# Layer norms with epsilon and negative mean on VectorE, one half tile on ScalarE, and three more modulations of layer 2 on TensorE

## The chip, the cores and the metric

The kernel runs on one core of a Trainium2 chip. The metric is the time of one execution in device microseconds. PE is TensorE (matmuls and transposes), DVE is VectorE, ACT is ScalarE, POOL is GpSimd, SP is SyncE, whose queue starts nearly all the transfers.

## The reference, cut to what matters

Four layers with four different mixers (pool, attention, a state-space model, a gated MLP) on a latent stream of 256 rows by 1024; in the first two layers a context stream of the same size goes through the same steps. Every layer norm normalises rows over 1024 columns, and every layer has six modulation vectors, each a product of a conditioning vector with a 1024 x 1024 matrix.

```python
def layer_norm(x, g, b):
    mu = jnp.mean(xf, axis=-1, keepdims=True)
    var = jnp.mean(jnp.square(xf - mu), axis=-1, keepdims=True)
    y = (xf - mu) * lax.rsqrt(var + LN_EPS) * g + b
...
for layer in range(DEPTH):                       # pool, attn, ssm, gmlp
    sh1, sc1, gt1, sh2, sc2, gt2 = jnp.split(silu(c) @ ada_w[layer] + ada_b[layer], 6)
    h_lat = modulate(x_lat, sh1, sc1)            # x * (1 + sc) + sh; h_ctx the same with c_ctx
    y_lat, y_ctx = mixer(h_lat, h_ctx)
    x_lat = layer_norm(ALPHA * x_lat + gt1 * y_lat, ln1_g, ln1_b)
    f_lat = conv_ffn(modulate(x_lat, sh2, sc2))
    x_lat = layer_norm(ALPHA * x_lat + gt2 * f_lat, ln2_g, ln2_b)
    # x_ctx goes through the same two norms in layers 0 and 1
```

## The kernel before, in words

The rows of the streams lie on the partitions in tiles `xa0` to `xa3` of 128 x 1024: tiles 0 and 1 are one stream, 2 and 3 the other. Layers 0 and 1 work on four tiles (`S=2`), layers 2 and 3 on two (`S=1`).

**Matmuls.** Every product is three matmuls of split operands, `mm3` (L229 to L231). A weight arrives by DMA as `raw`, ACT writes its high part `wH` (L170), and DVE, in some places POOL, its low part `wL` (L171).

**Modulations.** `ada_task(l, m)` makes modulation m of layer l (0 shift, 1 scale, 2 gate, 3 to 5 the same for the FFN). It loads eight slabs `araw` of 128 x 1024 (L327, issued from SP's queue, three buffers). Where `array(l, m)` holds, PE multiplies each slab straight from `araw` in `products` (L320): eight matmuls of 128 x 32 by 128 x 256, four column groups in two passes; it does so two slabs behind the load (`lag`). Otherwise DVE multiplies the slab by one column of the condition and adds it to an accumulator `adaS` (L337 for the first slab, L339 for the other seven), and PE sums `adaS` over the partitions at the end with one such group of eight. A gate adds a group for its bias. The tasks are background work of the matmul loops: some are advanced at each weight slab. Those of layer 2 with m = 0 to 4 run during the FFN of layer 1, about 855 to 1110 us; m = 0 and 1 already go to PE, m = 2, 3 and 4 to DVE.

**Second half of the two large FFNs.** While the FFN of layer 0 and again that of layer 1 go on, POOL builds tables for the state-space layer, group by group (`ef`, `efp`, L1176 to L1183, 128 x 512), which PE reads as background work (L1387, L1406). For layer 0's FFN this is 318 to 518 us, for layer 1's 977 to 1179 us.

**Layer norms.** `stats` collects sums per tile while the last matmuls of a stage land. `post(t, S)` then takes `rstd`: `bn_aggr` on DVE (mean and variance, L538), variance plus epsilon (L540) and the power of -0.5 (L541) on POOL. With `S=2` POOL goes on: the negative mean (L609), then both halves of the tile, `(x + nm) * rs` (L612). With `S=1` POOL makes `nm = -mean * rs` (L605), and `norm` runs the halves on ACT (L498, needs `nm`) and on DVE (L500, needs mean and `rs`). After that PE transposes the tile (`turn`, L555, or `turn_tile`, L506), and ACT and DVE modulate it into `hH`, `h` and `hL` (`modulate`, L582 to L591, or `modulate_tile`, L522 to L528). `finish` and the gated MLP's own norm use `rstd` too. The norms that `post` handles are the two of layers 0 and 1 (16 tiles), the two of layer 2 and the first of layer 3 (6 tiles).

**Order.** Each engine works through its queue in order. The order of DVE, ACT, POOL and SP is made by a planner that simulates a timeline, except inside `manual_schedule` blocks, where it is the order of the program. The whole pool layer is such a block. There `post(3)` comes ahead of `need((l, 3))` and `mod_coeffs` (L409 to L412, the coefficients `mA`, `mB` of `modulate`).

Of the kernel before, what the change touches and what calls it, by code (L numbers as in the profile page):

```python
# [7 lines left out]
F32 = mybir.dt.float32  # L8
# [3 lines left out]
ALU = mybir.AluOpType  # L12
# [9 lines left out]
EPS = 1e-5  # L22
# [43 lines left out]
class Trunk:  # L66
# [232 lines left out]

    def array(self, l, m):  # L300

        return l < 2 or l == 2 and m < 2

# [185 lines left out]
    def norm(self, t, engs):  # L491

        nc = self.nc
        mean, rs, nm = self.norms[t]
        for hf, e in enumerate(engs):
            x = self.xa[t][:, hf * 512:hf * 512 + 512]
            if e is nc.scalar:
                e.activation(x, x, AF.Identity, scale=rs, bias=nm)  # L498
            else:
                e.tensor_scalar(x, x, mean, rs, op0=ALU.subtract, op1=ALU.mult)  # L500

    def turn_tile(self, t):

# [30 lines left out]
    def rstd(self, st):  # L534

        nc = self.nc
        mv = self.t(self.sm, [128, 2], F32, "mv", 4)
        self.last_mv = nc.vector.bn_aggr(mv, st.rearrange("p a b -> p (a b)"))  # L538
        rs = self.t(self.sm, [128, 1], F32, "rs", 4)
        nc.gpsimd.tensor_scalar(rs, mv[:, 1:2], EPS, 1.0, op0=ALU.add, op1=ALU.mult)  # L540
        self.last_norm = nc.gpsimd.tensor_tensor(rs, rs, self.half, op=ALU.pow)  # L541
        return mv[:, 0:1], rs

# [55 lines left out]
    def post(self, t, S=2):  # L599

        G = self.nc.gpsimd
        mean, rs = self.rstd(self.st[t])
        if S == 1:
            nm = self.t(self.sm, [128, 1], F32, "nm", 4)
            G.tensor_scalar(nm, mean, rs, -1.0, op0=ALU.mult, op1=ALU.mult)  # L605
            self.norms[t] = mean, rs, nm
            return
        nm = self.t(self.sm, [128, 1], F32, "nm", 4)
        G.tensor_scalar(nm, mean, -1.0, 1.0, op0=ALU.mult, op1=ALU.mult)  # L609
        for hf in range(2):  # L610
            x = self.xa[t][:, hf * 512:hf * 512 + 512]
            self.last_norm = G.tensor_scalar(x, x, nm, rs, op0=ALU.add, op1=ALU.mult)  # L612

    def post_T(self, coef):

# [226 lines left out]
    def out_proj_steps(self, l, w, n_k, gates, norm, S, lhs, lead=0):  # L842


        NT = 2 * S
        made = {}
        def end():
            made["g"] = gates()
            made["n"] = norm()
        for hf in range(2):  # L850
            c0 = hf * 512
            P = 2 if S == 1 and hf else 1
            if hf:
                self.conv(l)
            if hf and S == 2:
                ahead = self.ahead([w for w, shape in self.first_up(l, 2)])
            def close(t, p, ps):
                if not made:
                    end()
                self.add_gated(t, c0 + p * 256, ps, made["g"][t // 2])  # L860
                if hf == 1 and p == P - 1:
                    self.post(t, S)
            yield from self.project_steps([(w[:, k:k + 2, c0:c0 + 512], (k, k + 1)) for k in range(0, n_k, 2)],
                                          lambda k, t: lhs(k, slice(t * 128, t * 128 + 128)), (0, n_k - 1), NT, 3 if hf else 0, P, close,
                                          made["n"][0] if P == 2 else None,
                                          self.first_up(l) if P == 2 and self.extra else (), 0 if hf else lead,
                                          (lambda: made["n"][0]) if S == 2 and hf else None)
        if S == 2:
            self.early = ahead
            self.post_T(made["n"][0])  # L870
        self.post_x(range(NT), made["n"][1])
# [813 lines left out]
    def gmlp_layer(self, l):  # L1685
# [5 lines left out]
        with ExitStack() as later:  # L1691
# [39 lines left out]
            for cp in range(8):  # L1731
# [7 lines left out]
                for j in range(2):  # L1739
# [12 lines left out]
                    for t in range(2):  # L1752
# [3 lines left out]
                    self.split(nH[:, :, cs], nL[:, :, cs], gt)  # L1756
            norm = self.pre_ln1(l)
            self.out_proj(self.out_proj_steps(l, I["gmlp_w_out"][0].rearrange("(k p) n -> p k n", p=128), 16, lambda: gates, lambda: norm, 1,
                          lambda k, ts: (nH[:, ts.start // 128, k * 128:k * 128 + 128], nL[:, ts.start // 128, k * 128:k * 128 + 128])))

# [229 lines left out]
```

## Time and profile before

| | |
|---|---|
| median of 3 runs | 1935.31 us (1934.91 to 1938.88) |
| the profiled execution's own time | 1940.46 us |
| its span in the trace | 1938.7 us |
| mean granted clock of PE | 0.96 |
| DVE busy | 1318.2 us (68%) |
| ACT busy | 781.3 us (40%) |

The profiled execution is one run of its own; its time lies 5.15 us above the median of the others. Durations of the trace belong to it. An engine's busy time is an average over stages that have different limits.

### The profile page before, as it was taken

What the parts mean: (1) busy time and instruction counts of PE and PEld (TensorE: products, weight loads), DVE (VectorE), ACT (ScalarE), POOL (GpSimd) and SP (SyncE); (2) the same over time, 40 slices, a digit from 0 to 9 for tenths busy, and PEclk for the clock granted to TensorE, in tenths of its full rate; (3) what the DMA queues carried; (4) which work ended last, traced back from release to release, by engine and by line L of the source; (5) the groups of instructions that cost most, each with busy time, mean ns of one, the idle gap of its engine ahead of it and who ended that gap; (6) DMA issues with size and microseconds to landing.
All of it is one profiled execution on the core that took longest, in us unless ns stands there. A gap on an engine that the chain in (4) does not pass through costs nothing.

```text
span 1938.7 us, 31709 instructions
## 1 busy us (share of the span) xinstructions
PE 1782.9 (92%) x12188; PEld 1466.6 (76%) x12188; DVE 1318.2 (68%) x1853; ACT 781.3 (40%) x1289; POOL 1080.3 (56%) x1040
## 2 busy tenths in 40 slices
PE   6899999899999999999989998688899988979997
PEld 4687676677789878777767776458798878979997
DVE  4565545546677767654676747987879798778666
ACT  2253223224346644422422332234654454436553
POOL 2278104989862335751189998647654444246643
PEclk8899999999999999999989999889899989989999
DMA  9555565565321124566656556865878765547662
GB/s 365 185 156 183 174 190 181 197 206 184 121 87 38 45 80 100 180 189 187 210 194 220 177 186 207 250 222 182 267 273 276 254 222 186 171 154 262 205 188 85
DMA packets 241785, 360.28 MB, mean 186 GB/s; under 512 B 43353, under 2 KB 164825, under 8 KB 241634
## 3 DMA queue, kind: packets, MB, share of 16 engines
q1 hardware_dynamic: 241634, 358.26, 57.2%
q8 instruction: 96, 1.57, 0.3%
q14 instruction: 55, 0.45, 0.1%
HBM read 330.92 MB, written 27.29 MB: 185 GB/s over the span
## 4 chain that ended last, share of the span: by engine, by line
PE 56%; POOL 21%; DVE 11%; issue 4%; DMA 4%; ACT 2%; SPq 0%; POOLq 0%; DVEq 0%; ACTq 0%
PE ps L229 15%; PE ps L230 14%; PE ps L231 14%; POOL ef L1178 2%; DVE wL L171 2%; POOL efp L1182 2%; POOL ef L1181 2%; POOL ef L1183 2%; POOL cv L1824 2%; POOL ef L1176 2%; POOL efp L1177 2%; PE sc L991 1%; PE ps L939 1%; PE ada L320 1%; PE pv L1046 1%
## 5 line engine op out<-in xcount | busy, mean ns | idle before, releaser
L171 DVE TENSOR_TENSOR wL<-raw,wH 128x1024 fp32r<-128x1024 f32 x292 | 422.8, 1453 | 197.2 <-ACT wH L170 189.9
L229 PE MATMUL ps<-hH,wH 128*128 128x256 f32 (+1 forms) x1568 | 524.2, 335 | 9.9 <-ACT wH L170 5.5
L170 ACT ACTIVATE wH<-raw 128x1024 fp32r<-128x1024 f32 x341 | 358.2, 1056 | 419.2 <-PE ps L231 218.3
L231 PE MATMUL ps<-hH,wL 128*128 128x256 f32 (+1 forms) x1568 | 516.8, 330 | 4.5 <-DVE wL L171 4.5
L230 PE MATMUL ps<-hL,wH 128*128 128x256 f32 (+1 forms) x1568 | 518.0, 331 | 1.6 <-DVE hL L528 1.1
L229 PEld LDWEIGHTS ps<-hH,wH 128*128 128x128 f32 x1568 | 301.7, 193 | 52.1 <-issue 8.9
L231 PEld LDWEIGHTS ps<-hH,wL 128*128 128x128 f32 x1568 | 301.5, 193 | 31.3 <-DVE wL L171 4.8
L230 PEld LDWEIGHTS ps<-hL,wH 128*128 128x128 f32 x1568 | 302.6, 193 | 26.7 <-POOL xa L633 1.3
L1824 POOL TENSOR_TENSOR cv<-cv,cv 128x512 f32<-128x512 f32 (+1 forms) x88 | 110.2, 1257 | 224.8 <-ACT cv L1823 224.8
L229 PE MATMUL ps<-wH,gH 128*128 128x512 f32 (+1 forms) x552 | 220.6, 400 | 9.0 <-DVE cv L1796 7.2
L231 PE MATMUL ps<-wH,gL 128*128 128x512 f32 (+1 forms) x552 | 213.9, 392 | 2.4 <-POOL gL L1828 2.3
L230 PE MATMUL ps<-wL,gH 128*128 128x512 f32 (+1 forms) x552 | 215.8, 391 | 0.0
L171 POOL TENSOR_TENSOR wL<-raw,wH 128x1024 fp32r<-128x1024 f32 x49 | 127.2, 2596 | 110.1 <-ACT wH L170 90.0
L1793 ACT ACTIVATE cv<-ps,cw 128x512 f32<-128x512 f32 (+1 forms) x176 | 115.9, 666 | 164.1 <-PE ps L231 138.9
L1794 DVE SCALAR_TENSOR_TENSOR cv<-ps,cw,cv 128x510 f32<-128x510 f32 (+1 forms) x176 | 106.5, 609 | 106.1 <-ACT cv L1793 105.9
L339 DVE SCALAR_TENSOR_TENSOR adaS<-araw,cond,adaS 128x1024 f32<-128x1024 f32 x70 | 117.0, 1671 | 36.2 <-DMA araw<-in_ada_w_dram 36.0
L229 PEld LDWEIGHTS ps<-wH,gH 128*128 128x128 f32 x552 | 106.0, 192 | 41.1 <-issue 15.8
L231 PEld LDWEIGHTS ps<-wH,gL 128*128 128x128 f32 x552 | 105.8, 192 | 26.8 <-POOL gL L1828 3.3
L230 PEld LDWEIGHTS ps<-wL,gH 128*128 128x128 f32 x552 | 106.1, 192 | 21.0 <-issue 0.2
L1796 DVE SCALAR_TENSOR_TENSOR cv<-ps,cw,cv 128x510 f32<-128x510 f32 (+1 forms) x176 | 106.7, 612 | 4.3
L540 POOL TENSOR_SCALAR rs<-mv 128x1 f32<-128x1 f32 x26 | 8.2, 314 | 165.5 <-DVE mv L538 165.0
L1827 ACT ACTIVATE gH<-cv 128x512 fp32r<-128x512 f32 (+1 forms) x88 | 45.9, 521 | 117.6 <-POOL cv L1824 117.6
(434 smaller groups left out, 3322.9 us busy)
## 6 DMA issues: line engine op xcount, KB each, us to landing
araw<-in_ada_w_dram SPq DMA_DIRECT2D x184, 512.0 KB
raw<-in_ffn_w_up_dram SPq DMA_DIRECT2D x176, 512.0 KB
raw<-in_ffn_w_down_dram SPq DMA_DIRECT2D x88, 512.0 KB
raw<-in_gmlp_w_in_dram SPq DMA_DIRECT2D x32, 512.0 KB
fD<-ef SPq DMA_DIRECT2D x16, 512.0 KB
eD<-eo SPq DMA_DIRECT2D x16, 512.0 KB
raw<-in_gmlp_w_out_dram SPq DMA_DIRECT2D x16, 512.0 KB
raw<-in_attn_w_qkv_dram SPq DMA_DIRECT2D x12, 512.0 KB
```

Source lines behind the costliest of these rows:

```text
L170: self.nc.scalar.activation(h, x, AF.Copy)
L171: (eng or self.nc.vector).tensor_tensor(l, x, h.bitcast(F32), op=ALU.subtract)
L229: mm(ps, lhsT=w[0], rhs=x[0], start=first, stop=False)
L230: mm(ps, lhsT=w[0], rhs=x[1], start=False, stop=False)
L231: mm(ps, lhsT=w[1], rhs=x[0], start=False, stop=last)
L339: nc.vector.scalar_tensor_tensor(a, raws[k], self.cond[:, k, r:r + 1], a, op0=ALU.mult, op1=ALU.add)
L1176: eng.tensor_tensor(out[0], a[0], b[0], op=ALU.mult)
L1793: nc.scalar.activation(c, p3, AF.Identity, scale=cw[:, 1, h:h + 1], bias=cw[:, 3, h:h + 1])
L1794: nc.vector.scalar_tensor_tensor(c[:, :, 1:], p3[:, :, :255], cw[:, 0, h:h + 1], c[:, :, 1:], op0=ALU.mult, op1=ALU.add)
L1796: nc.vector.scalar_tensor_tensor(c[:, :, :255], p3[:, :, 1:], cw[:, 2, h:h + 1], c[:, :, :255], op0=ALU.mult, op1=ALU.add)
L1824: nc.gpsimd.tensor_tensor(cv[0, j], cv[0, j], cv[1, j], op=ALU.mult)
L1827: nc.scalar.activation(gH, c0, AF.Copy)
```

## The change

1. `array`: modulations m = 2, 3 and 4 of layer 2 are now multiplied on PE from `araw`.
2. `rstd`: epsilon is added on DVE, with one instruction fewer for POOL; the power stays on POOL.
3. `post`: `nm = -mean * rs` is made on DVE, behind the power, for every tile, also with `S=2`. With `S=2` the halves go through `norm`: POOL with mean and `rs`, and ACT with `rs` and `nm` for the first half of tile 3.

```diff
     def array(self, l, m):
-        return l < 2 or l == 2 and m < 2
+        return l < 2 or l == 2 and m < 5
...
     def norm(self, t, engs):
...
-                e.tensor_scalar(x, x, mean, rs, op0=ALU.subtract, op1=ALU.mult)
+                i = e.tensor_scalar(x, x, mean, rs, op0=ALU.subtract, op1=ALU.mult)
+                if e is nc.gpsimd:
+                    self.last_norm = i
...
     def rstd(self, st):
...
-        nc.gpsimd.tensor_scalar(rs, mv[:, 1:2], EPS, 1.0, op0=ALU.add, op1=ALU.mult)
+        nc.vector.tensor_scalar(rs, mv[:, 1:2], EPS, None, op0=ALU.add)
         self.last_norm = nc.gpsimd.tensor_tensor(rs, rs, self.half, op=ALU.pow)
...
     def post(self, t, S=2):
         G = self.nc.gpsimd
         mean, rs = self.rstd(self.st[t])
-        if S == 1:
-            nm = self.t(self.sm, [128, 1], F32, "nm", 4)
-            G.tensor_scalar(nm, mean, rs, -1.0, op0=ALU.mult, op1=ALU.mult)
-            self.norms[t] = mean, rs, nm
-            return
         nm = self.t(self.sm, [128, 1], F32, "nm", 4)
-        G.tensor_scalar(nm, mean, -1.0, 1.0, op0=ALU.mult, op1=ALU.mult)
-        for hf in range(2):
-            x = self.xa[t][:, hf * 512:hf * 512 + 512]
-            self.last_norm = G.tensor_scalar(x, x, nm, rs, op0=ALU.add, op1=ALU.mult)
+        self.nc.vector.tensor_scalar(nm, mean, rs, -1.0, op0=ALU.mult, op1=ALU.mult)
+        self.norms[t] = mean, rs, nm
+        if S == 2:
+
+            self.norm(t, (self.nc.scalar if t == 3 else G, G))
```

## Rows read from the trace of the kernel before

**Rows 1.** The page, part 1: busy time, share and instructions of each engine.
```profile
PE 1782.9 (92%) x12188; PEld 1466.6 (76%) x12188; DVE 1318.2 (68%) x1853; ACT 781.3 (40%) x1289; POOL 1080.3 (56%) x1040
```

**Rows 2.** Busy time by stretch, equal parts of two FFNs: PE, PEld, DVE, ACT, POOL, PEclk, DMA.
```profile
269.90:498.70 228.80, 221.39 (x1530) 165.14 (x1530) 116.57 (x120) 79.51 (x118) 167.51 (x127) 0.99 0.59 188
928.10:1161.60 233.50, 215.13 (x1370) 167.58 (x1368) 153.82 (x145) 77.17 (x116) 179.35 (x127) 0.96 0.59 197
```

**Rows 3.** The same view of line L230 alone: the two stretches.
```profile
269.90:498.70 228.80, 105.17 (x267) 50.53 (x267) 0.99 0.59 188
928.10:1161.60 233.50, 107.51 (x267) 52.17 (x267) 0.96 0.59 197
```

**Rows 4.** The chain that ended last within each of the two stretches.
```profile
by line: PE ps L229 18.5%; PE ps L230 17.2%; PE ps L231 17.2%; POOL ef L1178 5.7%; PE ada L320 4.4%; POOL ef L1181 4.2%; POOL ef L1176 4.0%; POOL ef L1183 3.9%; POOL efp L1182 3.4%; DMA prm<-prmD 3.3%; POOL cv L1824 2.9%; DMA prmD<-big 2.8%
...
by line: POOL ef L1178 12.1%; POOL efp L1182 11.5%; POOL ef L1181 10.1%; POOL efp L1177 9.8%; POOL ef L1183 9.6%; POOL ef L1176 8.3%; DMA prm<-prmD 6.7%; POOL cv L1824 5.7%; PE ps L229 4.6%; PE ps L230 4.3%; PE ps L231 4.3%; DMA araw<-in_ad
```

**Rows 5.** Line L339 alone, in one stretch: time, DVE busy (instructions).
```profile
935.00:1182.00 247.00, 34.87 (x21) 0.96 0.57 192
```

**Rows 6.** Groups of line L320: the sums over partitions for layer 2's modulations.
```profile
L320 PE MATMUL ada<-adaS,ones x24: 379/391/404, 987.7 to 1109.2; 128*32 128x256 f32 x24
```

**Rows 7.** PE in order of time around one slab of a modulation.
```profile
905.42 0.39 PE L230 MATMUL ps<-hL,wH 128*128 128x512 f32 x1
905.65 0.39 PE L231 MATMUL ps<-hH,wL 128*128 128x512 f32 x1
905.97 0.64 PE L320 MATMUL ada<-araw,cond 128*32 128x256 f32 x8
...
906.87 0.39 PE L230 MATMUL ps<-hL,wH 128*128 128x512 f32 x1
```

**Rows 8.** One line of POOL's table work over the whole kernel: ns minimum/median/maximum.
```profile
L1182 POOL TENSOR_TENSOR efp<-prm x40: 1045/1396/2068, 329.5 to 1176.5; 128x512 f32<-128x512 f32 x40
```

**Rows 9.** Waits of SP's queue in the first stretch: total us, times, longest.
```profile
SPq L327 <- PE ada L320: 39.3, 14, 4.5
```

**Rows 10.** All engines in order of time: first norm of layer 0, tile 3.
```profile
78.12 0.17 DVE L409 TENSOR_SCALAR ada<-ada 128x16 f32<-128x16 f32 x1
...
78.46 2.34 POOL L171 TENSOR_TENSOR wL<-raw,wH 128x1024 fp32r<-128x1024 f32 x1 [4.64 <-ACT wH L170]
78.61 2.21 DVE L412 TENSOR_TENSOR mB<-mB,ada 128x16 f32<-128x16 f32 x1
...
80.86 3.76 ACT L582 ACTIVATE hH<-ps,mB,mA 128x256 fp32r<-128x256 f32 x8 [2.49 <-DVE mB L412]
81.90 0.19 POOL L540 TENSOR_SCALAR rs<-mv 128x1 f32<-128x1 f32 x1
...
82.17 0.55 POOL L541 TENSOR_TENSOR rs<-rs,half 128x1 f32<-128x1 f32 x1
...
87.76 0.55 PE L229 MATMUL ps<-hH,wH 128*128 128x256 f32 x1 [1.13 <-DVE h L588]
```

**Rows 11.** POOL and DVE in order of time: second norm of layer 0, tile 3.
```profile
536.28 1.03 POOL L540 TENSOR_SCALAR rs<-mv 128x1 f32<-128x1 f32 x1 [3.36 <-DVE mv L538]
537.40 1.05 POOL L609 TENSOR_SCALAR nm<-mv 128x1 f32<-128x1 f32 x1
538.41 1.53 POOL L541 TENSOR_TENSOR rs<-rs,half 128x1 f32<-128x1 f32 x1
540.05 1.52 POOL L612 TENSOR_SCALAR xa<-xa,nm,rs 128x512 f32<-128x512 f32 x2
...
536.11 3.43 DVE L171 TENSOR_TENSOR wL<-raw,wH 128x1024 fp32r<-128x1024 f32 x3
```

**Rows 12.** First norm of layer 3, tile 1, in order of time.
```profile
1721.68 0.66 DVE L522 TENSOR_SCALAR h<-ps,mA,mB 128x128 f32<-128x128 f32 x2
1722.72 0.55 DVE L500 TENSOR_SCALAR xa<-xa,mv,rs 128x512 f32<-128x512 f32 x1 [0.38 <-POOL rs L541]
...
1723.32 0.66 PE L506 MATMUL ps<-ident,xa 128*128 128x128 f32 x4 [2.03 <-DVE xa L500]
```

## Prediction

> **What bounds the kernel now.** I read the page first. PE is busy for 1782.9 of 1938.7 us, 92%, far ahead of DVE's 68% and POOL's 56% [rows 1]. So over the whole kernel PE is nearly the limit, and work added to PE costs time unless it falls into gaps that PE has anyway. The share is a mean over stages, though, and part 1 of the change acts in one stage, the second half of layer 1's FFN. So the second view is busy time by stretch. I laid two stretches of equal work beside each other: from the 900th to the 100th of the main matmuls counted from the FFN's end, once in layer 0's FFN and once in layer 1's. That they are equal is seen on one of the three products: 267 instructions of L230 in both [rows 3]. POOL has 127 instructions in both, table work for the state-space layer for the most part [rows 2]. What differs is the modulations. In layer 0's stretch all of them are on PE, so PE has 1530 instructions against 1370: 160 more, which are 20 slabs of eight. In layer 1's stretch those of m = 2, 3 and 4 are on DVE: 145 DVE instructions against 120, 153.82 us busy against 116.57. And yet layer 0's stretch is the shorter one: 228.80 us against 233.50 [rows 2]. The third view, the chain that ended last, says why: in layer 0's stretch three lines of matmuls lead it with 53% together, in layer 1's six lines of POOL's tables with 61% [rows 4]. In layer 1's stretch PE is idle for 18.37 us (233.50 less 215.13), in layer 0's for 7.41, and it is granted 0.96 of its clock against 0.99 [rows 2]. In layer 1's stretch PE waits for POOL, and POOL is slower there: 179.35 us busy for 127 instructions against 167.51, 11.84 more.
>
> The reader is to see that layer 0's stretch is a picture of layer 1's after the change, in the same trace.
>
> **Part 1, modulations from DVE to PE.** Removed: 24 DVE instructions of 128 x 1024 (three of L337, and the 21 of L339, which take 34.87 us of DVE [rows 5]), and three of PE's groups of eight over `adaS` [rows 6]. Added: 24 groups of eight on PE, one for each slab. Net: 21 groups more. What a group costs where PE is never idle, one place shows: from the start of one matmul of the main stream at 905.65 to the one two behind it at 906.87 is 1.22 us with a group between; without one, a step of this stream is 0.23 us (905.42 to 905.65), two are 0.46. The group costs 0.76 us [rows 7], and 21 of them 16.0 us: the upper bound of part 1.
>
> By the Trainium skill ("TensorE: Matmul & The Clock Gate", Part 3: Packing small matmuls) matmuls on different column tiles run side by side, so that four of them last about as long as one; by that rule the two passes of a group are worth two matmuls, and with half the columns of a main one that is about one step of the stream, 0.23 us, as an estimate 4.8 us for 21. The row says 0.76 us, and the row decides. The same section says that a weight load overlaps matmuls under way only where the row group differs, which speaks against this form, as the four column tiles share their rows.
>
> The lower bound: POOL sets the pace throughout, and gets rid of what DVE's large operations cost it. One line of its tables takes 1045 ns at the least and 2068 at the most with the same shape [rows 8], so an overlap can double it; the 11.84 us of busy time between the stretches [rows 2] is the total. So the ends are -11.84 and +16.0. Between these ends I go by the nearest row, which is the layer 0 stretch itself: -4.70 us. It has 20 groups more, the change adds 21; one more at the rate at which PE's busy time grew (221.39 less 215.13 over 20, 0.31 us) makes **-4.4 us**. That stretch also includes what the change does to the queues: with PE two slabs behind, SP's queue waits for PE to free an `araw`, 39.3 us in 14 waits [rows 9], with weight loads queued behind it. It is the shorter stretch all the same, with the DMA engines at 0.59 in both [rows 2].
>
> **Parts 2 and 3, the layer norms.** POOL loses an epsilon and an `nm` for each tile, 0.19 us apiece where nothing disturbs them [rows 10], and DVE gets both at about the same price (0.17 to 0.19 us, its smallest rows). The price that matters is another one: `nm` on DVE waits for POOL's power, and DVE takes its queue in order, so everything behind `nm` waits about 0.9 us: power 0.55, `nm` 0.19, epsilon 0.19.
>
> *First norm of layer 0, tile 3.* The order is the program's: `nm` stands ahead of the coefficients L409 to L412. Before, DVE did L409 at 78.12, and L412 ended at 80.82, when POOL's L171, which stands ahead of the power, had let it go; ACT's `hH` began at 80.86 [rows 10]. After, the power still waits for POOL's L171 and the instruction behind it (to 81.82), begins at 81.90, epsilon's place, and ends at 82.45; `nm` is done at about 82.7; the coefficients, at 0.17 each, at about 83.5. So `hH` begins 2.7 us later, and at the end of that chain PE stands idle for DVE's `h` at 87.76 [rows 10]. The half on ACT makes the tile itself earlier, but it is the coefficients that are late next. Bounds 0 and +3; I take **+2.5**, as the chain on DVE behind it has no gap.
>
> *Second norm of layer 0, tile 3.* Epsilon 1.03, `nm` 1.05, power 1.53 and then two halves: POOL is held by three L171 of DVE at the same time [rows 11]. After, epsilon is 0.19 on DVE, `nm` leaves POOL's chain and one half of 0.76 goes to ACT: 0.84 + 1.05 + 0.76 = 2.65 less. Against it, the three L171, low parts of weights, start about 1.1 us later behind `nm`. Bounds -3 and 0; I take half, **-1.3**. The second norm of layer 1 has the same shape with no contention (0.19 + 0.19 + 0.76 less, some 0.4 of it lost to the wait): -0.7. The first norm of layer 1 lies under matmuls: +0.2, to +1 without that cover.
>
> *The norms with `S=1`.* Here `nm` comes ahead of two L522 that DVE did while it waited: they ran at 1721.68, and L500 waited 0.38 us for the power at 1722.72 [rows 12]. After, the pair starts at about 1722.9, when the power (which L500 saw end just ahead of 1722.72) and `nm` are done, and L500 at 1723.55, 0.8 later; PE waits for just that instruction (2.03 us) [rows 12]. ACT gets `nm` earlier, but PE needs both halves: +0.7. Two other places have this shape, the first and second norm of layer 2; worked the same way, with the wait of tile 0 in it, they give +1.0 and +0.45. Together **+2.2**, bounds 0 and +4. The gated MLP's own norm and the last one only lose the epsilon on POOL, which there lies under a DVE operation: -0.5 and -0.3.
>
> Sum of the norms: 2.5 - 1.3 - 0.7 + 0.2 + 2.2 - 0.8 = **+2.1 us**.
>
> **Sum.** -4.4 + 2.1 = -2.3 us. The profiled execution took 1940.46 us (span 1938.7, 1.76 around it); it becomes 1938.2. It is 5.15 above the median of the runs shown, so against the median of 1935.31 I forecast **1933.0 us**. About 0.2%, 3.9 us, is what a measurement of this kernel can tell from no change.
>
> **Rivals.**
>
> *1. PE sets the pace and the groups aren't absorbed (slower).* For it: PE is at 92% over the kernel, and layer 0's stretch has only 7.41 us of idle PE left, so the stage is close to PE's limit with POOL just beneath [rows 2, 4]. Its place is the main matmul stream from about 935 us on, its price 0.76 us a group [rows 7]. All 21 unabsorbed give 16.0 + 2.1 = +18.1, 1953.4 us. It decides from where the stretch is longer by 1.8 us instead of shorter by 4.4, that is where 6.2 us more of the groups stay visible than in layer 0. Against it: the 20 groups in layer 0.
>
> *2. POOL sets the pace to the end.* The 11.84 us come back, and about half of the first eight groups, which run before POOL's tables begin (8 x 0.76 = 6.1 us), is paid: -11.84 + 3.0 + 2.1 = -6.7, 1928.6 us. For it: POOL's 61% of the chain now [rows 4]. Against it: in layer 0 PE takes over before POOL's gain is used up.
>
> The Trainium skill ("SBUF — State Buffer", SBUF: two separate sides) states that DVE and GpSimd share a port pair that is locked for a whole instruction, and that the other side stops. By that rule each removed L339 could free up to its own duration, 34.9 us as an estimate for the 21; the doubling in rows 8 agrees with the rule, while the 11.84 us show that few overlaps cost that much.
>
> *3. DVE's waits at the norms are covered.* If the coefficients and the L522 had slack that I don't see, the +2.5 and the +2.2 fall away, and the norms give -2.6: -4.4 - 2.6 = -7.0, 1928.3 us. Against it: at both places PE is idle for that very chain [rows 10, 12].
>
> *4. The planner orders other work anew.* New instructions change its simulated times; work elsewhere moves by a few us either way, centred on the forecast.
>
> **How the numbers follow.** The forecast has 0.42 (its own range 1930 to 1936), rival 1 0.19, rival 2 0.20, rival 3 0.11, rival 4 0.08. Faster by over 0.2% is below 1931.4: rivals 2 and 3 for the most part, some 0.26, with the lower edge of the forecast (0.11) and a third of rival 4: 0.40. Slower is above 1939.2: rival 1 with little left out, 0.17, and part of rival 4: 0.20. The rest, 0.40, is no change that can be measured. The range from 1926.5 to 1941 leaves out most of rival 1 and the far end of rival 2.
>
> **What would show it.** In the profile after: no L339 and no L337 before 1180 us, 21 more groups of L320 there; the chain in that stretch led by matmuls and not by POOL's tables; POOL's busy time for the same 127 instructions near 167.5 us, PE's idle time near 7; the stretch itself at 229 us. At the first norm of layer 0 ACT's `hH` some 2.7 us later and PE's restart with it; at the norms with one stream L500 behind two L522 that wait for `nm`. I am wrong if that stretch is longer than 235 us, or if a wait at a norm that I have priced under 1 us turns out above 2.

## The result and the profile after

The change made the kernel slower: 1948.69 us (1947.6 to 1950.84, four runs) against 1937.1 (1934.91 to 1939.25, four runs), ratio 1.0059 with a 95% interval of 1.0042 to 1.0076, or 11.6 us. The forecast was 1933.0 us in a range from 1926.5 to 1941.0. The profiled execution took 1949.58 us with a span of 1947.8.

The line of busy times on the page of the changed kernel answers to [rows 1]:

```profile
PE 1788.5 (92%) x12356; PEld 1465.4 (75%) x12356; DVE 1285.6 (66%) x1877; ACT 786.3 (40%) x1293; POOL 1087.3 (56%) x988
```

POOL has 52 instructions fewer and is still busy 7 us longer. That is the first sign of what went wrong, as the change takes work from POOL.

Part 1 did what was forecast. In layer 1's FFN, for the same 267 instructions of L230 as in [rows 3], the views of busy time (PE, PEld, DVE, ACT, POOL, PEclk, DMA share, GB/s) and of the chain now read:

```profile
929.10:1158.30 229.20, 222.23 (x1538) 166.06 (x1538) 114.79 (x122) 78.57 (x118) 166.27 (x128) 0.99 0.63 201
by line: PE ps L229 20.8%; PE ps L230 19.2%; PE ps L231 19.2%; PE ada L320 4.2%; POOL efp L1180 4.0%; POOL ef L1176 3.8%; POOL ef L1179 3.3%; POOL ef L1181 3.1%; POOL ef L1174 2.9%; DMA prmD<-big 2.6%; POOL cv L1822 2.4%; POOL efp L1175 2.3
```

229.20 us, where the forecast was 229 and the stretch took 233.50 before [rows 2]. PE's chain leads instead of POOL's [rows 4], POOL is busy for 166.27 us instead of 179.35, and PE idle for 6.97 us instead of 18.37. The granted clock is 0.99 instead of 0.96. The picture that layer 0's stretch gave of it was right within 2 us in every engine's column; only the DMA engines are busier than there, 0.63 against 0.59.

What went wrong is on POOL, in the halves that it normalises. The view of one line, of the kernel before and of the changed one (ns minimum/median/maximum):

```profile
L612 POOL TENSOR_SCALAR xa<-xa,nm,rs x32: 757/770/1356, 56.0 to 1194.3; 128x512 f32<-128x512 f32 x32
...
L500 POOL TENSOR_SCALAR xa<-xa,mv,rs x28: 2068/2076/2551, 51.9 to 1195.0; 128x512 f32<-128x512 f32 x28
```

A half tile takes POOL 2.08 us, and took 0.77 before. With two streams the halves go through `norm` now, which subtracts the mean and multiplies, while `post` used to add a negative mean and multiply. At the second norm of layer 1 the PE waits for it. Before, POOL and PE in order of time:

```profile
1187.08 1.52 POOL L612 TENSOR_SCALAR xa<-xa,nm,rs 128x512 f32<-128x512 f32 x2
...
1190.62 0.44 PE L555 MATMUL ps<-ident,xa 128*128 128x128 f32 x2 [1.09 <-POOL xa L612]
...
1194.32 2.82 PE L555 MATMUL ps<-ident,xa 128*128 128x128 f32 x12 [2.23 <-POOL xa L612]
```

After:

```profile
1179.76 4.14 POOL L500 TENSOR_SCALAR xa<-xa,mv,rs 128x512 f32<-128x512 f32 x2
1183.86 1.44 POOL L543 TENSOR_TENSOR rs<-rs,half 128x1 f32<-128x1 f32 x2
...
1186.80 10.30 POOL L500 TENSOR_SCALAR xa<-xa,mv,rs 128x512 f32<-128x512 f32 x5
...
1188.94 1.54 PE L557 MATMUL ps<-ident,xa 128*128 128x128 f32 x6 [4.55 <-POOL xa L500]
1190.99 1.54 PE L557 MATMUL ps<-ident,xa 128*128 128x128 f32 x6 [0.51 <-POOL xa L500]
1193.05 2.74 PE L557 MATMUL ps<-ident,xa 128*128 128x128 f32 x10 [0.52 <-POOL xa L500]
1197.16 1.54 PE L557 MATMUL ps<-ident,xa 128*128 128x128 f32 x6 [1.37 <-POOL xa L500]
```

Five halves stand in a row for 10.30 us, and PE's transposes wait for one after another. (Not all of PE's 4.55 us is the operation: POOL also takes the powers of three tiles, from 1183.86 us on, ahead of these halves.) The matmul just ahead of these transposes is 4.2 us earlier than in the trace of before, the gain of part 1; at 1210 us the work stands 1.8 us later.

The trace of before held the price. The gated MLP's norm uses the subtracting form on POOL already, on 128 x 1024, and the view of its line reads:

```profile
L1726 POOL TENSOR_SCALAR v<-v,mv,rs x2: 3987/4492/4998, 1618.4 to 1622.4; 128x1024 f32<-128x1024 f32 x2
```

About 2 us for each 512 columns; the prediction didn't look there.

### The profile page after: what moved, and what is told of

Read it like the earlier page. It is cut to its first block, busy times and chain, and to the rows that moved or that the text cites. A ratio compares the mean times of both kernels' runs of the same rounds, so it can differ in the third digit from the quotient of the medians.

```text
span 1947.8 us, 32032 instructions
## 1 busy us (share of the span) xinstructions
PE 1788.5 (92%) x12356; PEld 1465.4 (75%) x12356; DVE 1285.6 (66%) x1877; ACT 786.3 (40%) x1293; POOL 1087.3 (56%) x988
## 4 chain that ended last, share of the span: by engine, by line
PE 53%; POOL 17%; DVE 13%; DMA 7%; issue 7%; ACT 2%; SPq 1%; DVEq 0%; POOLq 0%; ACTq 0%
PE ps L229 14%; PE ps L230 14%; PE ps L231 14%; DMA araw<-in_ada_w_dram 3%; DVE wL L171 3%; DVE adaS L339 2%; POOL xa L500 2%; PE ada L320 2%; PE ps L937 1%; POOL cv L1822 1%; PE sc L989 1%; POOL ef L1176 1%; POOL efp L1180 1%; PE pv L1044 1%; POOL ef L1179 1%
## 5 line engine op out<-in xcount | busy, mean ns | idle before, releaser
L171 DVE TENSOR_TENSOR wL<-raw,wH 128x1024 fp32r<-128x1024 f32 x292 | 424.2, 1457 | 232.9 <-ACT wH L170 225.1
L230 PE MATMUL ps<-hL,wH 128*128 128x256 f32 (+1 forms) x1568 | 516.8, 330 | 0.0
L230 PEld LDWEIGHTS ps<-hL,wH 128*128 128x128 f32 x1568 | 302.1, 193 | 24.1 <-issue 1.0
L230 PE MATMUL ps<-wL,gH 128*128 128x512 f32 (+1 forms) x552 | 215.0, 390 | 0.0
L171 POOL TENSOR_TENSOR wL<-raw,wH 128x1024 fp32r<-128x1024 f32 x49 | 126.7, 2588 | 114.8 <-ACT wH L170 92.0
L230 PEld LDWEIGHTS ps<-wL,gH 128*128 128x128 f32 x552 | 105.4, 191 | 20.6
L543 POOL TENSOR_TENSOR rs<-rs,half 128x1 f32<-128x1 f32 x26 | 16.7, 645 | 157.6 <-DVE rs L542 157.6
L339 DVE SCALAR_TENSOR_TENSOR adaS<-araw,cond,adaS 128x1024 f32<-128x1024 f32 x49 | 82.3, 1681 | 10.0 <-DMA araw<-in_ada_w_dram 9.9
L1014 POOL TENSOR_SCALAR araw<-araw,den 128x512 f32<-128x512 f32 (+1 forms) x64 | 40.9, 655 | 85.8 <-ACT gate L1031 24.7
```

Source lines behind the costliest of these rows:

```text
L171: (eng or self.nc.vector).tensor_tensor(l, x, h.bitcast(F32), op=ALU.subtract)
L230: mm(ps, lhsT=w[0], rhs=x[1], start=False, stop=False)
L339: nc.vector.scalar_tensor_tensor(a, raws[k], self.cond[:, k, r:r + 1], a, op0=ALU.mult, op1=ALU.add)
L1014: nc.gpsimd.tensor_scalar(pt[:, e, i], pt[:, e, i], den[:, e, i:i + 1], 1.0, op0=ALU.mult, op1=ALU.mult)
```

## The experiments

Theory A: POOL's slow operation costs the time. Theory B: PE pays for the 21 groups, rival 1 of the prediction. Each ratio is against runs of the kernel before on the same chip; where a difference in us differs from that of the medians shown, it is worked out from the ratio.

**1. Part 1 alone** (e1).

```diff
-        return l < 2 or l == 2 and m < 2
+        return l < 2 or l == 2 and m < 5
```

> Part 1 alone: modulations 2 to 4 of layer 2 on PE, everything else as before. Theory A (the norms cost the time, since POOL takes 2.07 us for a half tile in the new form instead of 0.76): this kernel is 4 to 7 us faster than before, as the stretch in layer 1's FFN gained 5 to 6 us in the trace after. Theory B (PE pays for the 21 groups): 5 to 16 us slower than before.

1936.17 us against 1938.1, ratio 0.9989 (0.9975 to 1.0002): 2 us, and not certain. Theory B is out, but A's 4 to 7 us are not there at the end either; experiments 5 and 13 turn to that.

**2. The norms alone** (e2): as after, with `m < 2` again.

> Parts 2 and 3 alone: the layer norms as after, modulations as before. Theory A: 12 to 20 us slower than before, POOL's half tiles at 2.07 us as in the trace after. Theory B: about +2 us, the sum of the prediction, whatever POOL's half tiles take, since they lie under other work.

1951.86 us, ratio 1.0063 (1.0046 to 1.0080), 12.2 us. The norms carry the whole loss.

**3. Which form is slow** (e3), in the kernel before:

```diff
...
+            if t == 0:
+                self.last_norm = G.tensor_scalar(x, x, mean, rs, op0=ALU.subtract, op1=ALU.mult)
+            elif t == 1:
+                self.last_norm = G.tensor_scalar(x, x, nm[:, 0:1], rs, op0=ALU.subtract, op1=ALU.mult)
+            elif t == 2 or hf:
+                self.last_norm = G.tensor_scalar(x, x, nm[:, 0:1], rs, op0=ALU.add, op1=ALU.mult)
+            else:
+                self.last_norm = G.tensor_scalar(x, x, rs, nm[:, 1:2], op0=ALU.mult, op1=ALU.add)
```

> The kernel before with a different form of POOL's half tile (128 x 512) for each row tile: tile 0 subtracts the mean, read from the pair of mean and variance, and multiplies; tile 1 subtracts a copy of the mean from a tile of its own; tile 2 adds the negative mean (the form of before); tile 3 multiplies first and adds second in one half, and adds first in the other. If the operation subtract is slow (A1): about 2.07 us for tiles 0 and 1, 0.76 for tile 2 and both halves of tile 3. If the operand read from the pair of mean and variance is slow (A2): 2.07 us for tile 0 alone. If any form but add first and multiply second is slow (A3): also the first half of tile 3.

The view by line, in the order of the diff:

```profile
L618 POOL TENSOR_SCALAR xa<-xa,mv,rs x8: 2075/2078/2588, 52.1 to 1194.5; 128x512 f32<-128x512 f32 x8
L620 POOL TENSOR_SCALAR xa<-xa,nm,rs x8: 2072/2082/2612, 58.2 to 1202.2; 128x512 f32<-128x512 f32 x8
L622 POOL TENSOR_SCALAR xa<-xa,nm,rs x12: 772/779/2344, 68.2 to 1206.5; 128x512 f32<-128x512 f32 x12
L624 POOL TENSOR_SCALAR xa<-xa,rs,nm x4: 772/780/937, 79.8 to 1212.1; 128x512 f32<-128x512 f32 x4
```

It is the operation (A1): 2.08 us with subtract, wherever the mean lies, and 0.78 with add, in either order. The kernel was timed once, at 1963.76 us. That is longer than experiment 6 below, which has twice as many slow halves; one run, but it suggests that what a slow half costs the kernel depends on what stands around it.

**4. Multiply, then add** (e4), in the changed kernel:

```diff
-                i = e.tensor_scalar(x, x, mean, rs, op0=ALU.subtract, op1=ALU.mult)
-                if e is nc.gpsimd:
-                    self.last_norm = i
+                if e is nc.gpsimd:
+                    self.last_norm = e.tensor_scalar(x, x, rs, nm, op0=ALU.mult, op1=ALU.add)
+                else:
+                    e.tensor_scalar(x, x, mean, rs, op0=ALU.subtract, op1=ALU.mult)
```

> The changed kernel with one edit: POOL's half tiles are x * rs + nm (multiply first, add second) instead of (x - mean) * rs. Theory A: POOL's half tiles at about 0.77 us, and the kernel comes to 1930 to 1936 us, 3 us or more below the kernel before. Theory B: no gain over the changed kernel beyond 3 us, so about 1946 us or more.

1942.16 us, ratio 1.0010 (0.9994 to 1.0026), and the halves take POOL 0.77 us again (median). Of the 11.6 us some 9.5 are gone (1.0059 less 1.0010), but it doesn't beat the kernel before, and A's 1930 to 1936 us were missed: A named the largest cost, not all of them. In its trace the stretch of layer 0's second norm (as in the table below) takes 81.7 us, over 6 us more than before; PE waits there 3.0 us for ACT's half tile, which waits for `nm`, and 2.8 us for a low part of a weight from DVE, where before the longest wait was 2.6 us. PE's granted clock is lower there as well, 0.66 from 540 to 550 us against 0.83 and 1.00 in the two traces of before; how the 6 us divide between waits and clock was not tried.

**5. The kernel before, traced again** (e5), no edit.

> The kernel before, profiled a second time, to see what two traces of one program differ by in each stretch. If stretches of a trace repeat to under 1 us, the 3 to 4 us by which the gated MLP and the last FFN differ between the traces of before and after are an effect of the order in which the planner placed other work. If they differ by 2 to 4 us between the two traces of before, they are not to be read as an effect of the change.

1936.34 us. The table below lays stretches of several traces side by side. I found the same PE instruction at both ends of each stretch in every trace, and the numbers are differences of these start times, in us; the times in the first column are rounded. Two traces of one program differ by 0 to 2.3 us in a stretch.

| stretch (times of before) | before | again | after | 1 | 2 | 4 | 6 | 8 | 11 |
|---|---|---|---|---|---|---|---|---|---|
| 49 to 110, first norm, layer 0 | 60.8 | 61.9 | 63.1 | 61.5 | 63.2 | 64.3 | 62.2 | 63.5 | 63.3 |
| 505 to 580, second norm, layer 0 | 75.0 | 74.4 | 75.9 | 74.5 | 75.5 | 81.7 | 80.9 | 75.0 | 75.0 |
| 728 to 798, first norm, layer 1 | 69.9 | 69.9 | 73.1 | 69.9 | 73.1 | 70.3 | 75.4 | 71.0 | 70.9 |
| 890 to 1160, FFN, layer 1 | 270.0 | 268.9 | 265.7 | 265.2 | 268.7 | 265.4 | 269.3 | 262.7 | 268.3 |
| 1175 to 1210, second norm, layer 1 | 35.0 | 37.3 | 41.0 | 36.0 | 41.5 | 36.1 | 43.3 | 36.0 | 35.1 |
| 1310 to 1345, first norm, layer 2 | 35.0 | 34.3 | 34.6 | 34.6 | 34.1 | 34.3 | 35.3 | 34.4 | 34.7 |
| 1545 to 1565, second norm, layer 2 | 19.8 | 19.2 | 19.4 | 20.0 | 19.9 | 20.1 | 19.9 | 19.8 | 20.1 |
| 1581 to 1640, gated MLP, layer 3 | 58.8 | 58.3 | 62.5 | 62.3 | 62.3 | 60.4 | 60.7 | 61.8 | 61.8 |
| 1735 to 1805, FFN, layer 3 | 70.0 | 70.8 | 73.5 | 74.2 | 71.8 | 70.5 | 71.8 | 72.5 | 71.9 |

**6. Subtract alone** (e6), in the kernel before:

```diff
-        nm = self.t(self.sm, [128, 1], F32, "nm", 4)
-        G.tensor_scalar(nm, mean, -1.0, 1.0, op0=ALU.mult, op1=ALU.mult)
...
-            self.last_norm = G.tensor_scalar(x, x, nm, rs, op0=ALU.add, op1=ALU.mult)
+            self.last_norm = G.tensor_scalar(x, x, mean, rs, op0=ALU.subtract, op1=ALU.mult)
```

> The kernel before with POOL's half tiles as (x - mean) * rs instead of (x + nm) * rs, and no instruction for the negative mean; epsilon and everything else as before. If POOL's subtract is what made the change slow: 32 halves of 2.07 us, 8 to 13 us slower than before. If DVE's waits at the norms made it slow: within 3 us of before.

1958.47 us against 1936.13, ratio 1.0111 (1.0089 to 1.0134), 21.5 us: twice what was expected, though one instruction for each tile is saved. 32 halves at 1.3 us more are 42 us of POOL, so about half of it is exposed. With the rest of the norms' change around it the same form costs less (12.2 us in experiment 2); there four of the halves are on ACT and epsilon doesn't queue behind POOL's halves. Which of these two does it was not tried.

**7. Add in the gated MLP's norm too** (e7), on part 1 alone:

```diff
-                    e.tensor_scalar(v, v, *norms[t], op0=ALU.subtract, op1=ALU.mult)
+                    if i:
+                        nm = self.t(self.sm, [128, 1], F32, "nm", 4)
+                        e.tensor_scalar(nm, norms[t][0], -1.0, 1.0, op0=ALU.mult, op1=ALU.mult)
+                        e.tensor_scalar(v, v, nm, norms[t][1], op0=ALU.add, op1=ALU.mult)
```

(with the old line in the `else`).

> Part 1 alone (modulations on PE, norms as before), and in the gated MLP's own norm POOL's two tiles of 128 x 1024, which subtract the mean (3.99 and 5.00 us before), add a negative mean instead. If the operation is what costs: these two at about 1.5 us each, and 3 to 6 us below the kernel with part 1 alone (1936.2 against 1938.1 before), so 4 to 8 us below before. If PE's wait there is for another engine: no gain beyond the 2 us of part 1.

1938.00 us, ratio 1.0003 (0.9988 to 1.0018): no gain. The two tiles took 2.77 and 1.72 us instead of 5.00 and 3.99, but PE's longest wait there, for ACT's `nH`, went from 3.0 us in experiment 1 to 6.1. The traces show why. In experiment 1 ACT's first `nH` waits for DVE's `v`; here it waits for POOL's, although DVE's first `v` had been done for 2 us, and PE waits behind both:

```profile
1604.94 0.81 DVE L1731 TENSOR_SCALAR v<-v,mv,rs 128x1024 f32<-128x1024 f32 x1 [0.59 <-POOL rs L541]
...
1607.82 2.00 ACT L170 ACTIVATE nH<-v 128x1024 fp32r<-128x1024 f32 x2 [5.11 <-POOL v L1729]
...
1609.88 0.47 PE L229 MATMUL ps<-wsH,nH 128*128 128x128 f32 x1 [6.08 <-ACT nH L170]
```

So ACT's order took what the cheaper instructions gave; what they are worth with the old order was not tried.

**8. POOL makes its own negative mean** (e8), in the changed kernel, so that DVE waits for the power only in tile 3 and with one stream:

```diff
-        nm = self.t(self.sm, [128, 1], F32, "nm", 4)
-        self.nc.vector.tensor_scalar(nm, mean, rs, -1.0, op0=ALU.mult, op1=ALU.mult)
-        self.norms[t] = mean, rs, nm
+        if S == 1 or t == 3:
+            nm = self.t(self.sm, [128, 1], F32, "nm", 4)
+            self.nc.vector.tensor_scalar(nm, mean, rs, -1.0, op0=ALU.mult, op1=ALU.mult)
+            self.norms[t] = mean, rs, nm
         if S == 2:
...
+            G.tensor_scalar(ng, mean, -1.0, 1.0, op0=ALU.mult, op1=ALU.mult)
+            if t == 3:
+                self.norm(t, (self.nc.scalar,))
+            for hf in range(t == 3, 2):
...
+                self.last_norm = G.tensor_scalar(x, x, ng, rs, op0=ALU.add, op1=ALU.mult)
```

> The changed kernel, but with two streams POOL makes the negative mean itself and adds it, as before, so that DVE makes nm (and waits for the power) only for tile 3 and for the norms with one stream. If DVE's waits in tiles 0 to 2 cost the rest of what the norms lost (the kernel with multiply first and add second stood 1.9 us above before): 2 to 4 us below that one, at 1934 to 1938 with before at 1938. If the rest lies at tile 3 or in the norms with one stream: no change against that one, about 1940 to 1942.

1935.33 us, ratio 0.9998 (0.9982 to 1.0014). That is 2.3 us less than experiment 4 by the ratios (1.0010 to 0.9998), with intervals that overlap; the 6 us that experiment 4 lost at the second norm of layer 0 are gone from the trace.

**9 and 10. More modulations on PE** (e9: also m = 5 of layer 2; e10: also m = 0 to 2 of layer 3), both on experiment 8:

```diff
-        return l < 2 or l == 2 and m < 5
+        return l < 3
...
-        return l < 2 or l == 2 and m < 5
+        return l < 3 and m < 5 or l == 3 and m < 3 or l < 2
```

> The kernel with POOL's own negative mean, and modulation 5 of layer 2 on PE as well (it runs from about 1336 us on, in layer 2's last part, with one stream). If PE has gaps there as it has in layer 1's FFN, and DVE is what PE waits for: 2 to 5 us below that kernel, at about 1931 to 1933. If PE sets the pace there: 7 groups at 0.76 us, 5 us above it.

> The kernel with POOL's own negative mean, and modulations 0 to 2 of layer 3 on PE as well (from about 1386 us on, in layer 2's FFN). If DVE, busy there for nine tenths of the time, is what PE waits for: 3 to 8 us below that kernel. If PE sets the pace: 21 groups at up to 0.76 us, up to 16 us above it.

Experiment 9: 1933.21 us against 1936.61, ratio 0.9978 (0.9963 to 0.9994). Experiment 10: 1945.91, ratio 1.0046 (1.0029 to 1.0063). The same trade wins in one stage and loses in another. For layer 3's modulations the rival that PE sets the pace is the right one: over most of layer 2's FFN, for the same 318 instructions of L230, the views of PE (time, busy, granted clock, DMA share, GB/s) in experiments 8 and 10 are

```profile
1382.82:1533.44 150.62, 145.87 (x1010) 0.99 0.78 264
1381.90:1541.58 159.68, 159.68 (x1178) 1.00 0.77 250
```

PE has the 168 instructions of 21 groups more, is never idle, and the stretch is 9.1 us longer. Its busy time grew by 13.8 us, 0.66 for a group; the price of 0.76 from [rows 7] was about right where nothing absorbs it.

**11. The norms' change with the fast operation, without part 1** (e11): experiment 8 with `m < 2`.

> Parts 2 and 3 without part 1, and with two streams POOL makes the negative mean and adds it, as before; so it is the second experiment (12.2 us slower than before) with POOL's slow operation taken out. If that operation is the whole loss of the norms: within 3 us of before. If moving epsilon and nm to DVE costs something by itself: 3 us or more above before.

1939.94 us against 1937.4, ratio 1.0023 (1.0012 to 1.0033): 4.4 us slower. Against experiment 2 (1.0063) that is 0.4%, 7.8 us less; but two things differ between them, the operation and, in tiles 0 to 2, `nm`, which POOL makes again. The 4.4 us are what epsilon on DVE for all tiles, `nm` on DVE for tile 3 and for one stream, and the half on ACT cost together.

**12. All modulations of layer 2 on PE, norms as before** (e12): `return l < 3` in the kernel before.

> All modulations of layer 2 on PE, layer norms as in the kernel before: the fastest kernel so far (4.3 us below before) without any part of the norms' change. If the norms' change with the fast operation is worth nothing: within 2.5 us of that kernel, about 1930 to 1935 with before at 1936.6. If it is what made that kernel faster than part 1 alone: 1935 or more.

1928.33 us against 1937.4, ratio 0.9956 (0.9944 to 0.9968), 8.5 us faster than before. It beats both kernels. Experiment 9 differs from it only in the norms and stands 0.2% above it, with intervals that overlap a little.

**13. The last FFN without modulations on DVE** (e13): `return l < 3 or l == 3 and m == 5`.

> All modulations of layer 2 and the last one of layer 3 (m = 5, in layer 3's FFN) on PE, norms as before: the fastest kernel so far (1928.3 against 1937.4 before) and no L339 left in the last FFN. There part 1 lost 3 to 4 us against the two traces of before (74.2 us in the stretch that takes 70.0 and 70.8 before), with PE waiting for DVE's cv behind L339. If DVE's order there, with L339 ahead of cv, is the loss: that stretch comes back to 71 us or less, and the kernel to 1922 to 1927. If PE sets the pace there: up to 8 x 0.76 = 6 us slower than the fastest kernel, 1930 to 1934, and the stretch at 74 us or more.

1926.98 us against 1934.59, ratio 0.9960 (0.9947 to 0.9973): no faster than experiment 12 (the range expected was for a chip on which the kernel before takes 1937.4). The stretch did come back, 70.7 us where experiment 12 takes 73.4, and there is no wait for `cv` in it. The kernel did not gain it. Experiment 12 had lost its 3 us there with no wait for `cv` in its trace either, so what DVE's order is worth stays open; more on this stretch below.

## Why the prediction was wrong

**Part 1 was right in its place.** The forecast for the stretch was -4.4 us; the FFN of layer 1 takes 265.7 and 265.2 us with it (after, experiment 1) and 270.0 and 268.9 without. That is 3.2 to 4.9 us less, so the match with -4.4 is no better than two traces of one program allow. The nearest row, layer 0's FFN, was the right one to go by, between bounds of -11.84 and +16.0. SP's queue waits as in [rows 9], here in the stretch after, and the stretch is the shorter one all the same:

```profile
SPq L327 <- PE ada L320: 41.9, 15, 4.5
```

**The step that failed is the price of a half tile on POOL.** The prediction counted what moved: epsilon, `nm`, one half to ACT. It took the 28 halves that stay on POOL at their old 0.76 us and so put their change at nothing, though the diff changes their operation from add to subtract. Experiment 3 shows the price, 2.08 instead of 0.78 us. Two experiments change this operation and little else: experiment 4 takes it out of the changed kernel and gets 9.5 of the 11.6 us back, experiment 6 puts it into the kernel before and loses 21.5. The price of a half is settled; its share in the kernel's time goes with the order around it. The norms that were to be the gain, the second of layer 0 (-1.3) and of layer 1 (-0.7), lost about 1 and 4 to 6 us by the table, and the first of layer 1 (+0.2, "under matmuls") lost 3.2, because POOL's longer work there is no longer covered. A place at a norm priced under 1 us and found above 2 is one of the signs of being wrong that the prediction names. Experiment 8, with add, leaves about 1 us at that last place, and none at the two second norms.

**DVE's wait for the power was the right mechanism, mis-sized both ways.** The sum of the norms without the slow operation was +2.1 us. Experiment 4 against experiment 1 makes it roughly 4 (1.0010 less 0.9989); experiment 11, with less on DVE, measures +4.4 (2.3 to 6.4). The sum is not far off; its parts are. The views of the changed kernel in order of time show its parts. First norm of layer 0, tile 3:

```profile
77.72 0.57 POOL L543 TENSOR_TENSOR rs<-rs,half 128x1 f32<-128x1 f32 x1
78.33 0.21 DVE L606 TENSOR_SCALAR nm<-mv,rs 128x1 f32<-128x1 f32 x1 [5.85 <-POOL rs L543]
...
79.53 3.75 ACT L584 ACTIVATE hH<-ps,mB,mA 128x256 fp32r<-128x256 f32 x8
...
86.13 0.55 PE L229 MATMUL ps<-hH,wH 128*128 128x256 f32 x1 [4.04 <-ACT h L588]
```

DVE waits 5.85 us for POOL with the coefficients behind it, as the prediction has it: `hH` begins 1.81 us after the power (77.72 to 79.53), where it began 1.31 us ahead of it (80.86 and 82.17, [rows 10]). The +2.5 came out as +1.2 to +2.3 by the table (63.1 against 61.9 and 60.8). So rival 3, that these waits are covered, was wrong here. It was right for the terms for one stream, +2.2 together, which did not come: the two norms of layer 2 don't differ from before in the table by more than 0.3 us beyond what the two traces of before do. First norm of layer 3, tile 1:

```profile
1728.02 0.26 DVE L540 BATCH_NORM_AGGREGATE mv<-st 128x2 f32<-128x24 f32 x1
...
1729.13 0.21 DVE L606 TENSOR_SCALAR nm<-mv,rs 128x1 f32<-128x1 f32 x1 [0.66 <-POOL rs L543]
...
1729.90 0.54 DVE L500 TENSOR_SCALAR xa<-xa,mv,rs 128x512 f32<-128x512 f32 x1
...
1730.50 1.59 PE L508 MATMUL ps<-ident,xa 128*128 128x128 f32 x8 [2.95 <-DVE xa L500]
1735.32 0.58 PE L229 MATMUL ps<-hH,wH 128*128 128x256 f32 x1 [3.23 <-ACT wH L170]
```

and before, the first and the last of these:

```profile
1721.50 0.26 DVE L538 BATCH_NORM_AGGREGATE mv<-st 128x2 f32<-128x24 f32 x1
...
1728.77 0.58 PE L229 MATMUL ps<-hH,wH 128*128 128x256 f32 x1 [3.90 <-ACT wH L170]
```

From the tile's mean and variance to PE's transposes it is 2.48 us (1728.02 to 1730.50), and was 1.82 us (1721.50 to 1723.32, [rows 12]): 0.66 later, against +0.7 in the prediction. But to the next matmul of the main stream it is 7.30 us and was 7.27: that matmul waits for ACT's `wH`, before as after, and the wait swallows the delay (3.23 us left of 3.90). The prediction followed the chain one step too short: it stopped at the transposes and did not ask what the matmul behind them waits for.

The second norm of layer 0 shows an effect that I had not priced. With epsilon on DVE the planner may put other work in front of it:

```profile
536.70 0.26 DVE L540 BATCH_NORM_AGGREGATE mv<-st 128x2 f32<-128x24 f32 x1
536.87 2.29 DVE L171 TENSOR_TENSOR wL<-raw,wH 128x1024 fp32r<-128x1024 f32 x2
539.08 0.15 DVE L542 TENSOR_SCALAR rs<-mv 128x1 f32<-128x1 f32 x1
...
539.34 1.23 DVE L171 TENSOR_TENSOR wL<-raw,wH 128x1024 fp32r<-128x1024 f32 x1
540.49 0.20 DVE L606 TENSOR_SCALAR nm<-mv,rs 128x1 f32<-128x1 f32 x1
...
539.31 0.56 POOL L543 TENSOR_TENSOR rs<-rs,half 128x1 f32<-128x1 f32 x1 [5.37 <-DVE rs L542]
539.97 2.55 POOL L500 TENSOR_SCALAR xa<-xa,mv,rs 128x512 f32<-128x512 f32 x1
```

Two L171 stand between the mean and epsilon, 2.29 us for a step that takes 0.15. I had the three L171 wait behind `nm`; the planner put all three ahead of it, two of them ahead of epsilon too. From the end of the mean and variance to the power it is 2.35 us (536.96 to 539.31) and was 2.13 (536.28 to 538.41, [rows 11]), so the 1.89 us that epsilon and `nm` were to take off POOL's chain were spent here. The 0.76 us of the half that goes to ACT were lost to the slow operation: the one half left takes 2.55 us, the two before took 1.52.

**Rival 4 was too small.** Part 1's gain is only in part there at the end (2 us in experiment 1). Part 1 doesn't touch layer 3, yet the traces of experiment 1 and of the changed kernel are longer there in two places. In the gated MLP they take 62.3 and 62.5 us, the two of before 58.8 and 58.3. In layer 3's FFN the traces of experiment 1 and of the changed kernel take 74.2 and 73.5 us, the two of before 70.0 and 70.8. Waits of PE there (total, times, longest), the kernel before traced again and then experiment 1:

```profile
PE ps L231 <- DVE wL L171: 4.5, 1, 4.5
PE ps L229 <- ACT wH L170: 2.2, 1, 2.2
```

```profile
PE ps L231 <- DVE wL L171: 4.5, 1, 4.5
PE ps L229 <- DVE cv L1796: 3.6, 3, 2.1
```

In experiment 1 DVE's queue has a modulation step ahead of the two conv steps that make `cv`, here in order of time:

```profile
1765.64 3.40 DVE L339 SCALAR_TENSOR_TENSOR adaS<-araw,cond,adaS 128x1024 f32<-128x1024 f32 x1 [1.36 <-DMA araw<-in_ada_w_dram]
1768.96 0.47 DVE L1794 SCALAR_TENSOR_TENSOR cv<-ps,cw,cv 128x255 f32<-128x255 f32 x1
```

Experiment 6, which changes nothing past layer 1, shows the same wait and 71.8 us; experiment 4, with part 1 in it, takes 70.5. The waits are only part of the difference. PE in this stretch (time, busy, granted clock, DMA share, GB/s), before and in experiments 1 and 13:

```profile
1736.09:1806.26 70.17, 68.53 (x479) 0.97 0.80 266
...
1728.23:1802.59 74.36, 70.71 (x479) 0.94 0.78 254
...
1719.32:1790.22 70.90, 70.90 (x519) 0.99 0.80 267
```

In experiment 1 PE is idle for 2.0 us more and is busy 2.2 us longer with the same 479 instructions, at a granted clock of 0.94 against 0.97. In experiment 13 it is never idle, at 0.99. So the longer stretch goes with waits and with a lower clock in about equal parts; that one brings the other is not shown. An edit in one stage can cost some us in another, most likely by the planner's order; how much is not settled, since experiment 13 took the waits for `cv` away and the kernel did not get faster.

**Rivals 1 and 2.** Rival 1, that PE pays for the groups, is refuted for this stage and shown for layer 2's FFN (experiment 10). Rival 2, that POOL sets the pace to the end, is refuted for the part of the stage laid side by side: POOL got 13.1 us of busy time back (179.35 less 166.27), the stretch 4.3, with PE's lines leading the chain.

## What to carry to other kernels

Price every instruction that the diff rewrites by the new form, also one that stays on its engine: look for the new operation's own row anywhere in the trace, at any size. When one stage of the kernel already works as another will work after the change, lay the two stages side by side for equal work; here that gave the term of a stage to about 1 us between bounds 28 us apart. And follow a delay until it meets something that waits for something else.

## What the runs showed of the hardware

On POOL a `tensor_scalar` of fp32 on 128 x 512 with two operands for each partition takes 0.78 us with add and multiply in either order, and 2.08 us with subtract and multiply; on 128 x 1024 it was 1.72 against 3.99 us where it was shortest. DVE's half in the subtracting form takes 0.54 us (L500), as before; its price with add was not measured. I had expected one price for both operations on POOL. A group of eight small matmuls (128 x 32 by 128 x 256) added 0.66 us to PE's busy time where PE was never idle (experiment 10).
